# A top-k search whose scores get k's sign once, whose counts read one f32 tensor, and whose small operands lie in PSUM

## The chip, the cores and the metric

The kernel runs on one core of a Trainium2 chip. The core has five engines that each work through a queue of their own in order: TensorE (PE, matrix products into PSUM), VectorE (DVE), ScalarE (ACT), GpSimd (POOL) and SyncE (SP, which issues the transfers). They meet through semaphores. SBUF is the working memory, PSUM the eight banks into which TensorE writes. The metric is the time of one execution on the device in microseconds (us), median of several runs.

## What is computed

The reference is one inference step of a two-layer trunk for 1024 prompt rows and 64 sample rows, 1024 wide. Layer 0 projects the normalised rows into many column tiles; part of them feeds an attention over selected keys, another part a short gated convolution. Layer 1 is a gated unit with a mix over chunks. What matters here is the selection:

```
rel   = relu(einsum('bqhd,bsd->bqhs', qi, ki))
score = einsum('bqh,bqhs->bqs', wi, rel)
score = where(admissible, score, -inf)
top_val, top_idx = top_k(score, topk)        # 256 for the prompt, 144 for the sample
kg, vg = k[top_idx], v[top_idx]              # softmax over the chosen keys alone
```

The kernel never gathers. It finds the k-th largest score of each row exactly and adds 0 to the logits of the chosen keys and -1e30 to the others.

## The kernel before

**Rows and columns.** Scores exist for prompt blocks 2 to 7 (128 rows each, 384 to 1024 columns) and for the sample (576 columns). These seven row blocks lie side by side in one f32 tile `S` of 4800 columns. A column tile of a projection is 72 matrix products: three chunks of 364, 364 and 360 columns, 24 products each (8 pieces of the inner dimension, three products of the exact parts `w_hi`, `w_lo`, `ah`, `al`).

**The search** (`topk`, L488). It walks 31 rounds. In each round every row block counts how many of its scores are smaller than a trial value `cand`, compares the count with a limit (`m`, L571), makes a factor or step from that (`g`, L578 or L588) and moves `cand` (L579 or L590). A row whose k-th largest is negative is searched with its sign turned (`sgn`, +1 or -1 per row). The first 15 rounds (8 for the exponent, 7 for the mantissa) count in `bias`, a bf16 copy of the upper halves of the scores that already carries the sign (L529). The last 16 rounds count in `S` itself and multiply by the sign within the count (L531); there the trial value is a second input, spread over the columns.

**Who counts.** `GROUPS` (L81) makes three groups that go on by themselves. Group 0 (blocks of 512, 640, 768 and 576 columns) is counted by DVE. Group 1 (896 and 1024 columns) is counted by ACT as a sum of signs (L565, L568). Group 2 (384 columns) is counted by DVE in the first 15 rounds and by ACT afterwards. All the small steps are DVE's: three per group and round, on 1 to 4 columns. After the rounds, the blocks that ACT counted are counted once more on DVE (L595), six small steps make the threshold `T` (L598 to L603), and `mask` (L605) writes the additive mask of each block in six DVE instructions (L614 to L619).

**What runs beside it.** While DVE searches, PE computes the column tiles K, V, then GC, XIN and GZ of four convolution tiles (`pj`, L248), then Q1, Q2, Q3 and the first chunk and a half of GB0 as steps (L263; `BEFORE`, L89, is their number, 255 products). ACT copies each finished chunk out of PSUM (L784, L793) into `gc`, `z`, `bo` or `q` and makes `w_hi` of later tiles (L239). POOL makes `w_lo` (L240) and the convolution (L758 to L772). `gc` and `z` have one place each, so a convolution must be over before the next tile is copied there. Chunks rotate through five PSUM banks. Attention (L943 to L958) begins when the masks are there.

**What sets the order.** The order of the instructions within each engine is fixed when the program is built, by a timeline of the builder's own; the engines then run their queues in that order. So an ACT count that waits for a trial value from DVE holds up the copies that stand behind it in ACT's queue, and through the banks PE.

Of the kernel before, what the change touches and what calls it, by code (L numbers as in the profile page):

```python
# [9 lines left out]
F32 = mybir.dt.float32  # L10
# [13 lines left out]
TC = SEQ + 64      # prompt and sample columns  # L24
SO = SEQ           # first sample column
# [7 lines left out]
# chunks of columns: of the projections, and of those back to the residual, where a short one comes last  # L33
# [34 lines left out]
# widths of the score rows: prompt blocks 2..7, then the sample  # L68
# [24 lines left out]
def cut(n):  # L93
    """Equal pieces of at most one bank."""
    k = (n + 511) // 512
    return k, n // k


class Trunk:
# [5 lines left out]
    # ------------------------------------------------------------------ helpers  # L105
# [12 lines left out]
    # ------------------------------------------------------------------ constants  # L118
# [21 lines left out]
    # units of 512 modulation columns: u < 4 hold shift and scale of two k tiles each, 4 and 5 the gate  # L140
# [5 lines left out]
    def ada_steps(self, l, u, raw, halt=False):  # L146
        """A unit, a k tile at a step; with halt another step before the transposition."""
# [26 lines left out]
    def ada_late(self, pool):  # L174
        """The units that the index phase leaves room for, a k tile at a step; their loads run ahead."""
# [25 lines left out]
    def pace(self, after, n):  # L201
        """n steps of the side work, behind one of the matrix products."""
# [40 lines left out]
    def product(self, ps, w, c0, c1, kts=range(KT)):  # L243
        """ps [P, c1-c0] = W^T act, in three products of the exact parts."""
# [6 lines left out]
    def steps(self, w, evac, chunks=range(NCH), n=2, tag="pj"):  # L251
        """A projection, n matrix products at a step."""
# [90 lines left out]
            # 1/rms of every column on all partitions, in place of the sums  # L343
# [55 lines left out]
            # the place of the first tile's weights is free first  # L399
# [833 lines left out]
```

## Time and profile before

| what | value |
| --- | --- |
| time, median of 3 runs (lowest to highest) | 1203.1 us (1202.98 to 1203.14) |
| span of the profiled execution, first to last instruction | 1200.9 us |
| PE busy | 1098.8 us, 91% of the span |
| DVE busy | 729.0 us, 61% |
| ACT busy | 513.6 us, 43% |
| POOL busy | 460.2 us, 38% |
| chain that ended last | PE 61%, DVE 25%, ACT 5%, issue 3%, POOL 2%, DMA 2% |

Only the span of the profiled execution is shown; the 2.2 us between it and the median of the runs lie outside the first and last instruction. A share of busy time hides how long one instruction lasts: the DVE count of 576 columns in line L531 lasts 0.82 us in one round of this trace and 2.82 us in another. So the mean duration of one form, beside its shortest, says more than the share.

### The profile page before, as it was taken

Reading aid. Unit: us, or ns where it says so; the run is one execution under the profiler, and the core shown is the slowest. Engines: PE = TensorE matmul, PEld = TensorE weight load, DVE = VectorE, ACT = ScalarE, POOL = GpSimd, SP = SyncE. Lnnn points to the kernel's source line nnn. Section 1 sums busy time; section 2 is a strip of 40 time slices with the busy share of each in tenths; the row PEclk is TensorE's granted clock in tenths of the full one; section 3 lists DMA queues with packets and bytes.
Section 4 is the critical chain, followed back from the end, with each engine's and each line's share of the span. In section 5 each row is a group of like instructions: output and inputs, shape, how many; then the busy total and the mean of one; then the engine's idle time right before and its main releaser. Section 6 shows DMA issues by size and latency. Waiting matters only on the chain.

```text
span 1200.9 us, 18882 instructions
## 1 busy us (share of the span) xinstructions
PE 1098.8 (91%) x7255; PEld 1054.6 (88%) x7255; DVE 729.0 (61%) x1663; ACT 513.6 (43%) x964; POOL 460.2 (38%) x454
## 2 busy tenths in 40 slices
PE   5899999695959885999999899999999999999997
PEld 4799689595958885988999899999999999999996
DVE  5602899999999798776775534431159036346133
ACT  5332784645665525677775533431221211235110
POOL 3632322344647673544542324641133210245121
PEclk9999999898979896999999899999999999999998
DMA  9646401110101010000000350211111210121012
GB/s 362 279 167 220 168 2 53 73 36 19 36 18 36 19 58 14 19 19 19 19 19 19 114 175 1 71 36 36 36 59 40 84 37 19 52 77 65 1 62 88
DMA packets 26074, 81.84 MB, mean 68 GB/s; under 512 B 3072, under 2 KB 9984, under 8 KB 23552
## 3 DMA queue, kind: packets, MB, share of 16 engines
q1 hardware_dynamic: 25984, 80.63, 19.2%
q8 instruction: 57, 0.93, 0.3%
q14 instruction: 33, 0.27, 0.1%
HBM read 74.50 MB, written 6.12 MB: 67 GB/s over the span
## 4 chain that ended last, share of the span: by engine, by line
PE 61%; DVE 25%; ACT 5%; issue 3%; POOL 2%; DMA 2%; SPq 0%; POOLq 0%; DVEq 0%; ACTq 0%
PE pj L248 26%; PE op L248 15%; DVE cum L531 6%; PE pj L263 6%; DVE cum L529 5%; PE av L670 3%; PE logit_ps L632 3%; PE p_ps L662 2%; DVE m L571 2%; PE ada_ps L154 1%; DVE g L588 1%; PE sgu_ps L1048 1%; DVE cum L616 1%; PE first L319 1%; POOL w_lo L240 1%
## 5 line engine op out<-in xcount | busy, mean ns | idle before, releaser
L248 PE MATMUL pj<-ah,w_hi 128*128 128x364 f32 (+1 forms) x984 | 331.0, 336 | 34.4 <-ACT gc L784 33.0
L248 PE MATMUL pj<-al,w_hi 128*128 128x364 f32 (+1 forms) x984 | 328.3, 334 | 0.0
L248 PE MATMUL pj<-ah,w_lo 128*128 128x364 f32 (+1 forms) x984 | 327.5, 333 | 0.0
L240 POOL TENSOR_TENSOR w_lo<-w_raw,w_hi 128x1024 fp32r<-128x1024 f32 x63 | 160.9, 2556 | 380.8 <-ACT w_hi L239 356.8
L248 PEld LDWEIGHTS pj<-ah,w_hi 128*128 128x128 f32 x984 | 188.8, 192 | 36.6 <-ACT gc L784 33.9
L248 PEld LDWEIGHTS pj<-al,w_hi 128*128 128x128 f32 x984 | 188.8, 192 | 0.0
L248 PEld LDWEIGHTS pj<-ah,w_lo 128*128 128x128 f32 x984 | 188.5, 192 | 0.3 <-issue 0.2
L248 PE MATMUL op<-ah,w_lo 128*128 128x448 f32 (+2 forms) x384 | 126.7, 331 | 3.2 <-POOL w_lo L240 3.2
L248 PE MATMUL op<-al,w_hi 128*128 128x448 f32 (+2 forms) x384 | 127.0, 331 | 0.4 <-DVE al L278 0.3
L248 PE MATMUL op<-ah,w_hi 128*128 128x448 f32 (+2 forms) x384 | 127.3, 331 | 0.0
L239 ACT ACTIVATE w_hi<-w_raw 128x1024 fp32r<-128x1024 f32 x69 | 72.7, 1056 | 108.6 <-PE pj L248 79.1
L988 DVE SCALAR_TENSOR_TENSOR x<-op,mod,x 128x192 f32<-128x192 f32 (+2 forms) x64 | 30.5, 497 | 109.0 <-PE op L248 109.0
L263 PE MATMUL pj<-ah,w_hi 128*128 128x364 f32 (+1 forms) x288 | 96.2, 334 | 0.0
L263 PE MATMUL pj<-al,w_hi 128*128 128x364 f32 (+1 forms) x288 | 95.2, 331 | 0.0
L263 PE MATMUL pj<-ah,w_lo 128*128 128x364 f32 (+1 forms) x288 | 95.2, 331 | 0.0
L639 POOL TENSOR_SCALAR S<-S,sm 128x384 f32<-128x384 f32 (+8 forms) x68 | 50.8, 753 | 85.1 <-DVE sm L638 73.7
L248 PEld LDWEIGHTS op<-ah,w_lo 128*128 128x128 f32 x384 | 73.4, 191 | 5.5 <-POOL w_lo L240 3.5
L531 DVE SCALAR_TENSOR_TENSOR cum<-S,sgn,cand 128x512 bf16<-128x512 f32 (+3 forms) x67 | 76.7, 1145 | 1.5
L248 PEld LDWEIGHTS op<-al,w_hi 128*128 128x128 f32 x384 | 73.3, 191 | 3.2 <-DVE al L278 1.1
L248 PEld LDWEIGHTS op<-ah,w_hi 128*128 128x128 f32 x384 | 73.4, 191 | 2.0
L996 POOL TENSOR_TENSOR acc<-acc,sq 128x448 f32<-128x448 f32 (+2 forms) x40 | 40.0, 999 | 91.4 <-ACT sq L994 90.7
L278 DVE TENSOR_TENSOR ptl<-p_ps,pth 128x512 fp32r<-128x512 f32 (+1 forms) x88 | 54.4, 621 | 20.0 <-ACT pth L277 18.7
(251 smaller groups left out, 2120.1 us busy)
## 6 DMA issues: line engine op xcount, KB each, us to landing
w_raw<-in_w SPq DMA_DIRECT2D x53, 512.0 KB, 3.5
ada<-in_ada_w SPq DMA_DIRECT2D x19, 1024.0 KB, 9.1
w_raw<-in_wo SPq DMA_DIRECT2D x16, 512.0 KB, 3.4
x<-in_x SPq DMA_DIRECT2D x8, 544.0 KB, 6.6
bo<-in_ada_w SPq DMA_DIRECT2D x4, 1024.0 KB, 6.8
x<-in_x SPq DMA_DIRECT2D x1, 1792.0 KB, 8.8
out_y<-x SPq DMA_DIRECT2D x1, 1792.0 KB, 6.6
x<-in_x SPq DMA_DIRECT2D x1, 1536.0 KB, 9.2
```

The costliest lines, as they stand in the source:

```text
L239: nc.scalar.activation(hi, raw, AF.Copy)
L240: (nc.gpsimd if lo_eng == "pool" else nc.vector).tensor_sub(lo, raw, hi)
L248: last = self.nc.tensor.matmul(ps, wt[:, kt, :], at[:, kt, c0:c1], start=n == 0, stop=n == len(mms) - 1)
L263: self.nc.tensor.matmul(ps, wt[:, kt, :], at[:, kt, a:b], start=kt == 0 and i == 0, stop=kt == KT - 1 and i == 2)
L278: (lo_eng or self.nc.vector).tensor_sub(lo, src, hi)
L529: V.tensor_scalar(o, self.bias[:, span(j)], thr, 0.0, op0=OP.is_lt, op1=OP.add, accum_out=col(cv, j))
L531: V.scalar_tensor_tensor(o, self.S[:, span(j)], col(sgn, j), thr.to_broadcast([P, SW[j]]), op0=OP.mult, op1=OP.is_lt, accum_out=col(cv, j))
L632: mm = nc.tensor.matmul(pt[:, 0:w], lhs, keys[i][:, g, s], start=i == 0, stop=i == 1)
L639: nc.gpsimd.tensor_scalar(p, p, st[:, 3:4], 0.0, op0=OP.mult, op1=OP.add)
L670: mm = nc.tensor.matmul(av[:, 0:m], self.vs[0:r, vbase + j, g, :], t[0:r, o:o + m], start=j == 0 and i == 0, stop=j == nj - 1 and i == 1)
L988: nc.vector.scalar_tensor_tensor(x[:, t, a:b], ps[:, a:b], self.mod[l][:, 16 + t, j:j + 1], x[:, t, a:b], op0=OP.mult, op1=OP.add)
L996: nc.gpsimd.tensor_add(acc, acc, sq)
```

## The change

The bf16 copy of the upper halves goes. Once the signs are known, ACT multiplies `S` itself by `sgn`, seven copies in place, in the order of the groups. All 31 rounds then count in `S` in f32 with one form of instruction, a comparison with a scalar per row that adds up its results (`tensor_scalar` with an accumulator). ACT's counts use the constant scale -1 where they had a scale per row (`nsg`, which goes) or the half-step factor. Before the masks, ACT multiplies each block by `sgn` again, which gives the scores back. The limits `limd` and `lima`, the factor `g` and the table `step` move from SBUF to one PSUM bank (tag `av`); `m`, `cv`, `cand` and `T` stay in SBUF.

```
-        cv, m, sgn, nsg, limd, lima, T, cand, g, flag = (
-            t(n) for n in ("cv", "m", "sgn", "nsg", "limd", "lima", "T", "cand", "g", "flag"))
+        cv, m, sgn, limx, T, cand, flag = (t(n) for n in ("cv", "m", "sgn", "limx", "T", "cand", "flag"))
+        small = self.bank("av", "small")
+        limd, lima, g = (small[:, i * NSB:(i + 1) * NSB] for i in range(3))
+        step = small[:, 32:32 + steps * NSB].rearrange("p (s j) -> p s j", j=NSB)
...
-        def smaller(j, thr, first):
-            o = junks[0][:, 0:SW[j]]
-            if first:
-                V.tensor_scalar(o, self.bias[:, span(j)], thr, 0.0, op0=OP.is_lt, op1=OP.add, accum_out=col(cv, j))
-            else:
-                V.scalar_tensor_tensor(o, self.S[:, span(j)], col(sgn, j), thr.to_broadcast([P, SW[j]]),
-                                       op0=OP.mult, op1=OP.is_lt, accum_out=col(cv, j))
+        def smaller(j, thr):
+            V.tensor_scalar(junks[0][:, 0:SW[j]], self.S[:, span(j)], thr, 0.0, op0=OP.is_lt, op1=OP.add,
+                            accum_out=col(cv, j))
...
-        top = self.S.bitcast(BF).rearrange("p (n e) -> p n e", e=2)[:, :, 1]
-        for j in range(NSB):
-            if j in UPPER_ACT:
-                nc.scalar.activation(self.bias[:, span(j)], top[:, span(j)], AF.Copy, scale=col(sgn, j))
-            else:
-                V.tensor_scalar(self.bias[:, span(j)], top[:, span(j)], col(sgn, j), None, op0=OP.mult)
-        V.tensor_scalar(nsg, m, -2.0, 1.0, op0=OP.mult, op1=OP.add)
+        for j in sum((g[0] for g in GROUPS), ()):
+            nc.scalar.activation(self.S[:, span(j)], self.S[:, span(j)], AF.Copy, scale=col(sgn, j))
...
-                elif first:
-                    nc.scalar.activation(junks[1][:, 0:SW[j]], self.bias[:, span(j)], AF.Sign, scale=-1.0 - 2.0 ** -10,
-                                         bias=col(cand, j), accum_out=col(cv, j))
                 else:
-                    nc.scalar.activation(junks[1][:, 0:SW[j]], self.S[:, span(j)], AF.Sign, scale=col(nsg, j),
+                    nc.scalar.activation(junks[1][:, 0:SW[j]], self.S[:, span(j)], AF.Sign, scale=-1.0,
                                          bias=col(cand, j), accum_out=col(cv, j))
...
     def mask(self, pool, j):
+        self.nc.scalar.activation(sl, sl, AF.Copy, scale=self.sgn[:, p])
```

The order of the built program changes at three places that the prediction speaks of. Rows are number, line, operation, output and inputs, columns.

On ACT, the end of the search, before: `junk` are ACT's counts, `gc`, `z` and `q` the copies of finished chunks, and the count in row 227 is the last one.

```order
223 L568 ACTIVATE junk,cv<-S,cand,nsg 128x384
224 L568 ACTIVATE junk,cv<-S,cand,nsg 128x896
225 L568 ACTIVATE junk,cv<-S,cand,nsg 128x1024
226 L793 ACTIVATE z<-pj 128x364
227 L568 ACTIVATE junk,cv<-S,cand,nsg 128x384
228 L239 ACTIVATE w_hi<-w_raw 128x1024
229 L793 ACTIVATE z<-pj 128x296
230 L793 ACTIVATE z<-pj 128x64
231 L784 ACTIVATE q<-pj 128x364 x2
232 L239 ACTIVATE w_hi<-w_raw 128x1024
233 L784 ACTIVATE q<-pj 128x360
234 L784 ACTIVATE q<-pj 128x364 x2
```

And in the changed program: `S<-S,sgn` are the copies that give the scores back, and the last count stands in row 244.

```order
238 L238 ACTIVATE w_hi<-w_raw 128x1024
239 L772 ACTIVATE q<-pj 128x360
240 L601 ACTIVATE S<-S,sgn 128x576
241 L555 ACTIVATE junk,cv<-S,cand 128x896
242 L555 ACTIVATE junk,cv<-S,cand 128x1024
243 L772 ACTIVATE q<-pj 128x364
244 L555 ACTIVATE junk,cv<-S,cand 128x384
245 L601 ACTIVATE S<-S,sgn 128x384
246 L772 ACTIVATE q<-pj 128x364
247 L601 ACTIVATE S<-S,sgn 128x896
248 L601 ACTIVATE S<-S,sgn 128x1024
249 L238 ACTIVATE w_hi<-w_raw 128x1024
```

Before, the last count stood ahead of the last copies of XIN3 (`z`, 296 and 64 columns). Now seven copies of `q` chunks stand ahead of it: all three of Q1 and of Q2, and the first of Q3 (row 243).

On DVE, one round late in the search, before: four counts of group 0 and between them the small steps of all three groups.

```order
516 L531 SCALAR_TENSOR_TENSOR cum,cv<-S,sgn,cand 128x512
517 L531 SCALAR_TENSOR_TENSOR cum,cv<-S,sgn,cand 128x640
518 L531 SCALAR_TENSOR_TENSOR cum,cv<-S,sgn,cand 128x768
519 L531 SCALAR_TENSOR_TENSOR cum,cv<-S,sgn,cand 128x576
520 L571 TENSOR_TENSOR m<-cv,lima 128x2
521 L571 TENSOR_TENSOR m<-cv,limd 128x4
522 L588 SCALAR_TENSOR_TENSOR g<-m,step 128x2
523 L588 SCALAR_TENSOR_TENSOR g<-m,step 128x4
524 L571 TENSOR_TENSOR m<-cv,lima 128x1
525 L590 TENSOR_TENSOR cand<-cand,g 128x2
526 L590 TENSOR_TENSOR cand<-cand,g 128x4
527 L588 SCALAR_TENSOR_TENSOR g<-m,step 128x1
```

And a late round in the changed program, where `small` is the PSUM bank.

```order
535 L528 TENSOR_SCALAR cum,cv<-S,cand 128x512
536 L528 TENSOR_SCALAR cum,cv<-S,cand 128x640
537 L558 TENSOR_TENSOR m<-cv,small 128x2
538 L528 TENSOR_SCALAR cum,cv<-S,cand 128x768
539 L575 SCALAR_TENSOR_TENSOR small<-m,small 128x2
540 L528 TENSOR_SCALAR cum,cv<-S,cand 128x576
541 L577 TENSOR_TENSOR cand<-cand,small 128x2
542 L558 TENSOR_TENSOR m<-cv,small 128x1
543 L575 SCALAR_TENSOR_TENSOR small<-m,small 128x1
544 L577 TENSOR_TENSOR cand<-cand,small 128x1
545 L558 TENSOR_TENSOR m<-cv,small 128x4
```

The number of instructions in a round is the same; each of them now has at most one tensor input in SBUF, and the steps of group 1 stand between the counts of group 0.

On DVE in the masks of the changed program, one product for the convolution branch (`bo<-bo,pj`, the first chunk of GB0) stands in row 575.

```order
573 L603 TENSOR_SCALAR bias<-S,T 128x640
574 L603 TENSOR_SCALAR bias<-S,T 128x768
575 L894 TENSOR_TENSOR bo<-bo,pj 128x364
576 L603 TENSOR_SCALAR bias<-S,T 128x896
577 L603 TENSOR_SCALAR bias<-S,T 128x1024
```

Before, it came behind the last instruction of the masks.

## Rows read from the trace of the kernel before

**Rows 1.** Stages: us, busy time of each engine (instructions), granted clock, DMA.
```profile
187.60:202.00 14.40, 14.38 (x87) 14.35 (x88) 13.55 (x29) 2.90 (x4) 4.62 (x4) 1.00 0.31 104
187.60:444.70 257.10, 211.42 (x1200) 209.60 (x1201) 244.57 (x646) 133.79 (x241) 130.84 (x123) 0.90 0.12 40
461.80:682.50 220.70, 211.97 (x1399) 199.91 (x1399) 156.30 (x481) 156.18 (x330) 99.19 (x95) 0.98 0.08 28
...
412.40:461.00 48.60, 33.80 (x204) 33.35 (x202) 48.25 (x49) 8.81 (x15) 29.27 (x22) 0.88 0.11 36
412.40:429.20 16.80, 16.80 (x103) 16.80 (x102) 16.70 (x24) 3.79 (x6) 15.94 (x17) 1.00 0.10 33
```

**Rows 2.** Waits of PE from 180 to 462: total us, times, longest.
```profile
PE pj L248 <- ACT gc L784: 33.0, 3, 13.0
PE logit_ps L632 <- DVE sm L634: 15.0, 1, 15.0
```

**Rows 3.** Groups on DVE, 180 to 462: busy us, mean ns of one, idle before.
```profile
L531 DVE SCALAR_TENSOR_TENSOR cum<-S,sgn,cand 128x576 bf16<-128x576 f32 x16 | 20.7, 1295 | 0.1
...
L571 DVE TENSOR_TENSOR m<-cv,lima 128x2 f32<-128x2 f32 x31 | 13.0, 418 | 6.4 <-ACT junk L568 6.4
...
L529 DVE TENSOR_SCALAR_CACHE_REDUCE cum<-bias,cand 128x576 bf16<-128x576 bf16 x15 | 12.2, 811 | 0.4
...
L590 DVE TENSOR_TENSOR cand<-cand,g 128x2 f32<-128x2 f32 x22 | 3.5, 157 | 0.1
...
L614 DVE TENSOR_SCALAR_CACHE_REDUCE bias<-S,T,kneg 128x576 bf16<-128x576 f32 x1 | 0.9, 869 | 0.0
```

**Rows 4.** DVE in order of time: start us, us, instruction.
```profile
188.52 0.66 DVE L538 TENSOR_SCALAR sgn<-m 128x7 f32<-128x7 f32 x1
...
202.04 0.75 DVE L529 TENSOR_SCALAR_CACHE_REDUCE cum<-bias,cand 128x512 bf16<-128x512 bf16 x1
...
206.76 0.74 DVE L529 TENSOR_SCALAR_CACHE_REDUCE cum<-bias,cand 128x512 bf16<-128x512 bf16 x1
...
289.93 0.74 DVE L531 SCALAR_TENSOR_TENSOR cum<-S,sgn,cand 128x512 bf16<-128x512 f32 x1
...
304.84 0.75 DVE L531 SCALAR_TENSOR_TENSOR cum<-S,sgn,cand 128x512 bf16<-128x512 f32 x1
...
309.12 0.75 DVE L531 SCALAR_TENSOR_TENSOR cum<-S,sgn,cand 128x512 bf16<-128x512 f32 x1
...
311.90 2.82 DVE L531 SCALAR_TENSOR_TENSOR cum<-S,sgn,cand 128x576 bf16<-128x576 f32 x1
...
314.66 1.95 DVE L571 TENSOR_TENSOR m<-cv,lima 128x2 f32<-128x2 f32 x1
...
385.45 1.75 DVE L531 SCALAR_TENSOR_TENSOR cum<-S,sgn,cand 128x512 bf16<-128x512 f32 x1
...
402.97 0.62 DVE L531 SCALAR_TENSOR_TENSOR cum<-S,sgn,cand 128x384 bf16<-128x384 f32 x1
...
412.43 0.67 DVE L614 TENSOR_SCALAR_CACHE_REDUCE bias<-S,T,kneg 128x384 bf16<-128x384 f32 x1
...
460.80 0.31 DVE L619 TENSOR_SCALAR bias<-bias 128x576 bf16<-128x576 bf16 x1
```

**Rows 5.** POOL in order of time, beside the two long DVE rows of 311.90 and 314.66.
```profile
311.10 3.02 POOL L240 TENSOR_TENSOR w_lo<-w_raw,w_hi 128x1024 fp32r<-128x1024 f32 x1 [11.01 <-ACT w_hi L239]
314.07 2.52 POOL L760 TENSOR_TENSOR z<-z,gc 128x1024 f32<-128x1024 f32 x1
```

**Rows 6.** Line L166, a small DVE sum that reads PSUM: ns shortest, median, longest.
```profile
L166 DVE TENSOR_TENSOR mod<-ada_ps,adab x20: 144/153/167, 23.8 to 149.6; 128x4 f32<-128x4 f32 x16, 128x8 f32<-128x8 f32 x4
```

**Rows 7.** ACT: a group of its counts, and the copy of Q3's first chunk.
```profile
L568 ACT ACTIVATE junk<-S,cand,nsg 128x1024 bf16<-128x1024 f32 x16 | 19.8, 1239 | 0.4
...
430.50 0.48 ACT L784 ACTIVATE q<-pj 128x364 f32<-128x364 f32 x1 [2.70 <-PE pj L263]
```

**Rows 8.** Line L615, the second mask instruction: ns shortest, median, longest.
```profile
L615 DVE TENSOR_SCALAR bias<-S,T x7: 568/1506/1855, 418.8 to 426.8; 128x384 bf16<-128x384 f32 x1, 128x512 bf16<-128x512 f32 x1, 128x640 bf16<-128x640 f32 x1, 128x768 bf16<-128x768 f32 x1
```

More of the change, by code (lines that the diff above doesn't have):

```diff
@@ L83 @@
 COL = {j: n for n, j in enumerate(sum((g[0] for g in GROUPS), ()))}
-UPPER_ACT = (4, 5)
 SPANS = [slice(min(COL[j] for j in g[0]), max(COL[j] for j in g[0]) + 1) for g in GROUPS]
@@ L513, in topk @@
         nc.gpsimd.memset(tiny, 2.0 ** -126)
-        cv, m, sgn, nsg, limd, lima, T, cand, g, flag = (
-            t(n) for n in ("cv", "m", "sgn", "nsg", "limd", "lima", "T", "cand", "g", "flag"))
-        self.T, self.cv = T, cv
+        cv, m, sgn, limx, T, cand, flag = (t(n) for n in ("cv", "m", "sgn", "limx", "T", "cand", "flag"))
+        self.T, self.cv, self.sgn = T, cv, sgn
         junks = [self.cum, pool.tile([P, SEQ], BF, name="junk")]
+        small = self.bank("av", "small")
+        limd, lima, g = (small[:, i * NSB:(i + 1) * NSB] for i in range(3))
+        step = small[:, 32:32 + steps * NSB].rearrange("p (s j) -> p s j", j=NSB)
         def span(j):
@@ L523, in col @@
             return v[:, COL[j]:COL[j] + 1]
-        def smaller(j, thr, first):
-            o = junks[0][:, 0:SW[j]]
-            if first:
-                V.tensor_scalar(o, self.bias[:, span(j)], thr, 0.0, op0=OP.is_lt, op1=OP.add, accum_out=col(cv, j))
-            else:
-                V.scalar_tensor_tensor(o, self.S[:, span(j)], col(sgn, j), thr.to_broadcast([P, SW[j]]),
-                                       op0=OP.mult, op1=OP.is_lt, accum_out=col(cv, j))
+        def smaller(j, thr):
+            V.tensor_scalar(junks[0][:, 0:SW[j]], self.S[:, span(j)], thr, 0.0, op0=OP.is_lt, op1=OP.add,
+                            accum_out=col(cv, j))
         for j in range(NSB):
-            V.tensor_scalar(junks[0][:, 0:SW[j]], self.S[:, span(j)], 0.0, 0.0, op0=OP.is_lt, op1=OP.add,
-                            accum_out=col(cv, j))
+            smaller(j, 0.0)
         V.tensor_tensor(m, cv, lims[:, 1, :], op=OP.is_le)
         V.tensor_scalar(sgn, m, 2.0, -1.0, op0=OP.mult, op1=OP.add)
-        top = self.S.bitcast(BF).rearrange("p (n e) -> p n e", e=2)[:, :, 1]
-        for j in range(NSB):
-            if j in UPPER_ACT:
-                nc.scalar.activation(self.bias[:, span(j)], top[:, span(j)], AF.Copy, scale=col(sgn, j))
-            else:
-                V.tensor_scalar(self.bias[:, span(j)], top[:, span(j)], col(sgn, j), None, op0=OP.mult)
-        V.tensor_scalar(nsg, m, -2.0, 1.0, op0=OP.mult, op1=OP.add)
-        for lim, i in ((limd, 0), (lima, 2)):
-            V.tensor_sub(lim, lims[:, i + 1, :], lims[:, i, :])
-            V.tensor_mul(lim, lim, m)
-            V.tensor_add(lim, lim, lims[:, i, :])
-        for j in range(NSB):
-            smaller(j, col(tiny, j), True)
+        for j in sum((g[0] for g in GROUPS), ()):
+            nc.scalar.activation(self.S[:, span(j)], self.S[:, span(j)], AF.Copy, scale=col(sgn, j))
+        for lim, i in ((limd, 0), (lima, 2)):
+            V.tensor_sub(limx, lims[:, i + 1, :], lims[:, i, :])
+            V.tensor_mul(limx, limx, m)
+            V.tensor_add(lim, limx, lims[:, i, :])
+        for j in sum((g[0] for g in GROUPS), ()):
+            smaller(j, col(tiny, j))
         V.tensor_tensor(flag, cv, limd, op=OP.is_le)
@@ L555, in topk @@
         V.tensor_scalar(cand, tiny, exps[0], None, op0=OP.mult)
-        step = pool.tile([P, steps, NSB], F32, name="step")
         def count(n, first):
@@ L562, in count @@
                 if not act:
-                    smaller(j, col(cand, j), first)
-                elif first:
-                    nc.scalar.activation(junks[1][:, 0:SW[j]], self.bias[:, span(j)], AF.Sign, scale=-1.0 - 2.0 ** -10,
-                                         bias=col(cand, j), accum_out=col(cv, j))
+                    smaller(j, col(cand, j))
                 else:
-                    nc.scalar.activation(junks[1][:, 0:SW[j]], self.S[:, span(j)], AF.Sign, scale=col(nsg, j),
+                    nc.scalar.activation(junks[1][:, 0:SW[j]], self.S[:, span(j)], AF.Sign, scale=-1.0,
                                          bias=col(cand, j), accum_out=col(cv, j))
@@ L594, in topk @@
             if j in ACT_ROWS:
-                smaller(j, col(cand, j), False)
+                smaller(j, col(cand, j))
             else:
```

## The prediction

> **What bounds the kernel now.** I read the stages first, then PE's waits, then DVE's groups by form, and last DVE and POOL side by side in time. PE is the engine that the kernel as a whole is made for: from 461.8 us, where attention begins, to 682.5 it works 211.97 of 220.70 us [rows 1], and nothing in that stage or behind it is touched by the change. The place that can give time is the search and the masks, 188 to 461 us. There DVE is busy 244.57 of 257.10 us and PE only 211.42 [rows 1]. PE waits 33.0 us for ACT's copies of `gc` out of its banks and, once its 255 steps are through, 15.0 us for the masks [rows 2]. ACT is late with `gc` since a count stands ahead of the copy in its queue and waits for DVE's trial value. So DVE sets the pace, directly at the end and through ACT's queue on the way.
>
> DVE is "busy" but not working all the time. An undisturbed round takes 206.76 - 202.04 = 4.72 us among the first 15 and 309.12 - 304.84 = 4.28 among the last 16 [rows 4]. The first 15 took 289.93 - 202.04 = 87.9 us, 17.1 more than 15 x 4.72. The next 15 took 385.45 - 289.93 = 95.5 us, 31.3 more than 15 x 4.28. That is 48 us in which DVE stands. Where: at 311.90 a count that otherwise takes 0.82 us takes 2.82, while POOL's `w_lo` runs from 311.10 to 314.12; the comparison behind it takes 1.95 us, until POOL's next instruction ends at 316.59 [rows 4, 5]. Both forms read two tensors from SBUF, as POOL's do. The count of line L529, with one tensor input and a scalar, does not suffer: its 15 counts of 576 columns have a mean of 811 ns, the 16 of line L531 one of 1295 [rows 3].
>
> **The change, part by part.**
>
> *Counts in f32 by one form.* 67 counts of the two-input form become the form with one input. Is it as fast in f32 as in bf16? Line L614 is this form on f32: 869 ns for 576 columns against 811 in bf16 [rows 3], and it ran while POOL was busy 15.94 of 16.80 us [rows 1]. So I take 0.81 to 0.87 us per 576 columns in every round, at most 7% (0.3 us a round) above the undisturbed one, and no standing.
>
> [...]
>
> *Small operands in PSUM.* Nine of the small steps in a round (`m`, `g`, `cand` for three groups) read or write `limd`, `lima`, `g` or `step`. Each now reads at most one tensor from SBUF, which takes the standing away as it does for the counts: `m` of group 1 has a mean of 418 ns [rows 3], and a sum that reads PSUM never took more than 167 [rows 6]. What does PSUM cost? That sum has a median of 153 ns, one from SBUF alone a mean of 157 [rows 3, 6], so I take nothing more. A write of such a small result to PSUM has no row; bounds: nothing, or another whole duration, 0.16 us.
>
> [...]
>
> *Signs.* Before, `sgn` is ready at 189.2 and the first count of round 1 starts at 202.04 [rows 4]. After, the first of ACT's copies (about 0.7 us) goes ahead of seven counts that start as each block is ready: about 6.8 us by the rates above, the rest of the copies beside them. Round 1 starts near 197, 5 us earlier. On ACT a count loses its scale per row and does not become slower than 1239 ns for 1024 columns [rows 7].
>
> *DVE's sum.* 197 + 15 x 4.72 + 16 x 4.28 = 336 us, and one more ACT round of about 4 for the groups that ACT counts: 340.
>
> *What is late next.* In the new order ACT's last count stands behind the copy of Q3's first chunk, so the search can't end before PE has that chunk. PE needs 14.40 us for 87 products, 0.1655 each [rows 1]. From 187.6 it has 13 tiles of 72, Q1 and Q2 with 144 and 24 of Q3: 1104 products, 182.7 us, and 1 for nine transposes: 371.3 us. That is 31 us behind DVE's sum, so PE paces the search now, and DVE has about 1 us of room in each round. It is also what hides the 0.3 us of the f32 counts, and ACT's seven copies at the start.
>
> PE's standing goes with DVE's: the whole stage has 1200 products and transposes [rows 1], about 198 us, and took 257; 59 us were lost in waits and the slow clock after them (0.90 granted on the mean). 33.0 of them are the three waits on `gc` [rows 2]; these vanish when ACT is ahead. Of the other 26 I leave 3, since the first transposes of V still wait for ACT and DVE (bounds 0 and 26).
>
> *The end.* 371.3 + 3 of waits, 1.3 for copy and last count, then `m`, `g`, `T`, three recounts and six small steps. These took 412.43 - 402.97 = 9.5 us from the recounts on, with two recounts held up; undisturbed about 5.7 with the steps before them. Masks start at 381. They took 48.6 us beside 29.27 us of POOL [rows 1]. Line L615 would need about 7 x 0.57 = 4.0 instead of its mean of 1.2 and more (8.6 in all, seven of them; its shortest is 568 ns [rows 8]); its excess of 4.6 came beside a convolution that by then is over. The other mask lines meet `w_lo` and the query stacks as before. I take 44 (41 to 48.6). The copies that return the scores are finished block by block ahead of the masks, the last two after Q3's second chunk, 4 us behind the first and 6 us ahead of their use. The GB0 product that now stands in the masks needs PE's product 1176, 387 us with the same waits, and is reached at about 390; it adds its 0.5. Attention starts at 425.5 instead of about 461.3 [rows 4]: 36 us.
>
> Behind it PE is full and keeps its 220.7 us [rows 1]; the order there is slightly changed, which I price at 0 (up to 3 either way). Span 1200.9 - 36 = 1165; with the 2.2 us around it: **1167 us**, against the median 1203.1.
>
> **The rivals.**
>
> *PSUM is dear.* Nine steps fit into the room of 1 us per round while each costs under 0.11 us more. At the upper bound, 0.16, DVE's sum grows by 31 x 9 x 0.16 = 45 us, 14 above PE's: 1181. At 0.28 nothing is left of the gain: 1203. The row on reading speaks against it, on writing there is none.
>
> [...]
>
> *Standing stays, the form with one input meets POOL too* when it reads f32. Then 48 us stay on DVE and only the 5 at the start are won: about 1198. L614 beside a busy POOL speaks against it.
>
> *PE keeps part of its waits,* since the convolution on POOL, not the search, holds `gc`: each microsecond kept moves the end by one. With 10 to 26 kept: 1174 to 1190.
>
> *Slower: the search is chained to PE.* Its last count used to need PE's XIN3, and now needs Q3's first chunk. If PE ran as before, that chunk would be copied at 430.5 [rows 7]; count, closing and masks then end at 430.5 + 1.3 + 5.7 + 44 = 482, 20 us later than now: 1223. It decides once more than 39 of PE's 59 lost microseconds stay. For it speaks that the order does put the copy first; against it that the three `gc` waits follow DVE's long rounds.
>
> **How the numbers follow.** The forecast gets 0.72, with a range of its own of 1156 to 1178 (masks 41 to 48.6, PE's waits 0 to 8, 3 for the order behind). PE keeping 10 us or more: 0.12. PSUM dear: 0.06. Standing stays: 0.03. f32 at half the rate: 0.02. Slower through the chain to PE: 0.05. Within 0.2% (about 2.4 us, what a measurement of this kernel can't tell from no change) falls a piece of the last cases and of dear PSUM, 0.03. That makes 0.92 faster, 0.03 the same, 0.05 slower. The range of 1154 to 1187 leaves out the slow end of the rivals, about 0.15, and a little below.
>
> **What would show it.** Right: rounds of 4.7 to 5.9 us with hardly one above 7, no DVE count over 1.1 us; `m` of group 1 under 200 ns; PE without 10 us waits on `gc`, its granted clock near 1.00 from 230 to 385; ACT idle before the copies of chunks, waiting for PE; the last count right behind a `q` copy at 370 to 380; masks done near 425; PE waiting 25 to 35 us for them. Wrong: small steps near 0.3 us each (PSUM), counts of 576 columns near 1.5 us or more (f32 or POOL), PE still 30 us late at its first Q1 chunk.

## The result, and the profile after

The changed kernel takes 1161.8 us (median of four runs, 1160.1 to 1162.2) against 1203.0 for the kernel before on the same chip: a ratio of 0.966, 95% interval 0.964 to 0.967. The forecast was 1167, the range 1154 to 1187. The profiled execution has a span of 1160.5 us, 40.4 less than before.

Four stages, read off DVE's order of time in both traces [rows 4], show where the time came from:

| from, to | before, us | after, us | difference |
| --- | --- | --- | --- |
| start of the signs (`sgn`) to round 1 | 13.52 | 11.57 | -1.95 |
| round 1 to the first recount | 200.93 | 174.64 | -26.29 |
| first recount to the first mask instruction | 9.46 | 4.39 | -5.07 |
| masks, to the first logits of attention | 49.04 | 38.57 | -10.47 |

That is 43.8 us. The stretch ahead of the signs, where the code is the same, took 2.3 us longer in this execution (190.84 against 188.52), and the time from the first logits to the end 1.1 longer (740.49 against 739.43): 40.4 remain.

DVE of the changed kernel in order of time: start us, us, instruction.

```profile
190.84 0.67 DVE L534 TENSOR_SCALAR sgn<-m 128x7 f32<-128x7 f32 x1
191.43 0.78 DVE L540 TENSOR_TENSOR limx<-limx,m 128x7 f32<-128x7 f32 x1
192.24 2.35 DVE L541 TENSOR_TENSOR small<-limx,lims 128x7 f32<-128x7 f32 x1
...
194.91 0.74 DVE L528 TENSOR_SCALAR_CACHE_REDUCE cum<-S,tiny 128x512 bf16<-128x512 f32 x1
...
202.41 0.75 DVE L528 TENSOR_SCALAR_CACHE_REDUCE cum<-S,cand 128x512 bf16<-128x512 f32 x1
...
365.57 0.75 DVE L528 TENSOR_SCALAR_CACHE_REDUCE cum<-S,cand 128x512 bf16<-128x512 f32 x1
...
375.31 0.16 DVE L558 TENSOR_TENSOR m<-cv,small 128x2 f32<-128x2 f32 x1 [5.17 <-ACT junk L555]
...
377.05 0.61 DVE L528 TENSOR_SCALAR_CACHE_REDUCE cum<-S,cand 128x384 bf16<-128x384 f32 x1
...
381.44 0.67 DVE L602 TENSOR_SCALAR_CACHE_REDUCE bias<-S,T,kneg 128x384 bf16<-128x384 f32 x1
...
420.01 0.28 DVE L622 CUSTOM_DVE_ANT_0 S<-logit_ps,corner 128x128 f32<-128x128 f32 x1
```

The reader is to see three things. The masks start at 381.44, the forecast's 381. Two small steps that read two tensors from SBUF still stand at the start (line L540 for 0.78 us, and L541 for 2.35; their second pair, some 3 us later, takes 0.17 each). And at the end of the search DVE waits 5.17 us for ACT's last counts. The groups on DVE (busy us, mean ns of one, idle before) show that the counts and the small steps no longer stand in the rounds:

```profile
L528 DVE TENSOR_SCALAR_CACHE_REDUCE cum<-S,cand 128x576 bf16<-128x576 f32 x31 | 25.1, 811 | 0.0
...
L558 DVE TENSOR_TENSOR m<-cv,small 128x2 f32<-128x2 f32 x31 | 4.8, 155 | 19.7 <-ACT junk L555 19.4
...
L575 DVE SCALAR_TENSOR_TENSOR small<-m,small 128x4 f32<-128x4 f32 x23 | 3.8, 165 | 0.5
```

The f32 count of 576 columns takes 811 ns, to the nanosecond what the bf16 count took [rows 3]; `m` of group 1 takes 155 instead of 418. What DVE lost to standing it now partly waits for ACT: 19.7 us ahead of `m`. PE's stages (busy time of each engine, granted clock, DMA) and its waits from 180 to 470:

```profile
187.60:390.30 202.70, 201.72 (x1217) 201.25 (x1215) 173.74 (x627) 140.18 (x255) 117.09 (x125) 1.00 0.15 51
390.30:421.90 31.60, 0.94 (x4) 0.50 (x2) 29.68 (x36) 2.02 (x6) 2.87 (x3) 0.56 0.00 0
...
400.00:420.00 20.00, 0.00 (x0) 0.00 (x0) 19.79 (x21) 0.14 (x1) 0.00 (x0) 0.50 0.00 0
...
381.44:420.00 38.56, 9.01 (x57) 8.80 (x55) 38.25 (x50) 4.07 (x7) 8.22 (x5) 0.66 0.05 17
420.00:641.50 221.50, 211.74 (x1399) 199.03 (x1399) 156.00 (x484) 157.36 (x334) 97.46 (x95) 0.98 0.08 28
```

```profile
PE logit_ps L620 <- DVE sm L622: 31.9, 2, 29.9
PE pj L247 <- ACT w_hi L238: 1.0, 1, 1.0
```

PE works 201.72 of 202.70 us at a granted clock of 1.00, where before it lost some 59 us in this stage at 0.90 on the mean [rows 1]; the three waits on `gc` [rows 2] are gone. In their place stand 31.9 us of waiting for the masks, 29.9 of them in one piece, in which PE does nothing; from 400 to 420 the granted clock is 0.50.

### The profile page after: what moved, and what is told of

Its sections match the earlier page's. It is cut to its first block, busy times and chain, and to the rows that moved or that the text cites. A ratio compares the mean times of both kernels' runs of the same rounds, so it can differ in the third digit from the quotient of the medians.

```text
span 1160.5 us, 18892 instructions
## 1 busy us (share of the span) xinstructions
PE 1087.5 (94%) x7255; PEld 1044.7 (90%) x7255; DVE 670.2 (58%) x1657; ACT 519.3 (45%) x976; POOL 440.1 (38%) x454
## 3 DMA queue, kind: packets, MB, share of 16 engines
q1 hardware_dynamic: 25984, 80.63, 19.7%
## 4 chain that ended last, share of the span: by engine, by line
PE 81%; DVE 7%; ACT 5%; POOL 3%; issue 3%; DMA 1%; SPq 0%; POOLq 0%; DVEq 0%; ACTq 0%
PE pj L247 40%; PE op L247 15%; PE pj L262 9%; PE av L658 3%; PE logit_ps L620 2%; PE p_ps L650 2%; PE ada_ps L153 2%; PE sgu_ps L1036 1%; PE score_ps L427 1%; PE first L318 1%; POOL w_lo L239 1%; POOL hf L329 1%; DVE cum L604 1%; PE score_ps L428 1%; DVE al L277 1%
## 5 line engine op out<-in xcount | busy, mean ns | idle before, releaser
L247 PE MATMUL pj<-ah,w_hi 128*128 128x364 f32 (+1 forms) x984 | 326.0, 331 | 1.0 <-ACT w_hi L238 1.0
L247 PE MATMUL pj<-al,w_hi 128*128 128x364 f32 (+1 forms) x984 | 323.8, 329 | 0.0
L247 PE MATMUL pj<-ah,w_lo 128*128 128x364 f32 (+1 forms) x984 | 323.1, 329 | 0.0
L239 POOL TENSOR_TENSOR w_lo<-w_raw,w_hi 128x1024 fp32r<-128x1024 f32 x63 | 158.0, 2510 | 341.3 <-ACT w_hi L238 336.4
L247 PEld LDWEIGHTS pj<-ah,w_hi 128*128 128x128 f32 x984 | 185.0, 188 | 2.0 <-ACT w_hi L238 1.3
L247 PEld LDWEIGHTS pj<-ah,w_lo 128*128 128x128 f32 x984 | 184.8, 188 | 0.3 <-issue 0.2
L247 PEld LDWEIGHTS pj<-al,w_hi 128*128 128x128 f32 x984 | 185.0, 188 | 0.0
L528 DVE TENSOR_SCALAR_CACHE_REDUCE cum<-S,cand 128x512 bf16<-128x512 f32 (+5 forms) x142 | 119.0, 838 | 2.0
L262 PE MATMUL pj<-ah,w_hi 128*128 128x364 f32 (+1 forms) x288 | 96.0, 334 | 0.0
L262 PE MATMUL pj<-ah,w_lo 128*128 128x364 f32 (+1 forms) x288 | 95.2, 330 | 0.0
L262 PE MATMUL pj<-al,w_hi 128*128 128x364 f32 (+1 forms) x288 | 95.1, 330 | 0.0
L555 ACT ACTIVATE junk<-S,cand 128x896 bf16<-128x896 f32 (+2 forms) x78 | 77.7, 996 | 24.4 <-DVE m L558 20.6
L620 PE MATMUL logit_ps<-kp,qst 128*128 128x384 f32 (+5 forms) x192 | 49.6, 366 | 33.2 <-DVE sm L622 32.6
```

What stands on the lines that cost most here:

```text
L239: (nc.gpsimd if lo_eng == "pool" else nc.vector).tensor_sub(lo, raw, hi)
L247: last = self.nc.tensor.matmul(ps, wt[:, kt, :], at[:, kt, c0:c1], start=n == 0, stop=n == len(mms) - 1)
L262: self.nc.tensor.matmul(ps, wt[:, kt, :], at[:, kt, a:b], start=kt == 0 and i == 0, stop=kt == KT - 1 and i == 2)
L528: V.tensor_scalar(junks[0][:, 0:SW[j]], self.S[:, span(j)], thr, 0.0, op0=OP.is_lt, op1=OP.add, accum_out=col(cv, j))
L555: nc.scalar.activation(junks[1][:, 0:SW[j]], self.S[:, span(j)], AF.Sign, scale=-1.0, bias=col(cand, j), accum_out=col(cv, j))
L620: mm = nc.tensor.matmul(pt[:, 0:w], lhs, keys[i][:, g, s], start=i == 0, stop=i == 1)
```

## The experiments

Each kernel ran beside the kernel before on the same chip, so ratios compare best; the changed kernel has 0.9657 (0.9643 to 0.9671).

| kernel | median us | ratio, 95% interval |
| --- | --- | --- |
| after, small operands in SBUF | 1184.0 | 0.9833 (0.9815 to 0.9850) |
| before, small operands in PSUM | 1182.4 | 0.9822 (0.9807 to 0.9836) |
| after, late counts with two SBUF inputs | 1176.8 | 0.9772 (0.9753 to 0.9791) |
| before, `w_lo` twice | 1238.6 | 1.0289 (1.0274 to 1.0304) |
| after, `w_lo` twice | 1169.4 | 0.9729 (0.9716 to 0.9743) |
| after, return copies on POOL | 1159.4 | 0.9646 (0.9629 to 0.9663) |
| after, 120 products ahead | 1175.0 | 0.9771 (0.9749 to 0.9793) |
| after, second mask instruction adds up | 1161.0 | 0.9656 (0.9643 to 0.9669) |
| after, 320 products ahead | 1157.0 | 0.9625 (0.9612 to 0.9638) |
| after, masks late | 1159.1 | 0.9632 (0.9612 to 0.9652) |
| after, masks late, 320 products ahead | 1156.6 | 0.9603 (0.9581 to 0.9625) |

**Which of the two parts removes the standing.** First the changed kernel with its small operands back in SBUF.

```
-        small = self.bank("av", "small")
+        small = pool.tile([P, 200], F32, name="small")
```

> The changed kernel with limd, lima, g and step back in SBUF; counts and signs stay as changed. Theory (a small step with two tensors in SBUF stands while POOL reads SBUF): in the kernel before, the small steps of a round took about 35 us more in all than at 0.15 to 0.17 us each; that comes back. The comparison m of group 1 has a mean of 300 ns or more (155 in the changed kernel), the counts keep 0.81 us per 576 columns, DVE becomes the pacer again, masks start 8 to 25 us after 381, time 1168 to 1185 us. Rival (the standing belonged to the two-input counts, small steps only queued behind them): m under 200 ns, time within 4 us of 1161.8.

```profile
L528 DVE TENSOR_SCALAR_CACHE_REDUCE cum<-S,cand 128x576 bf16<-128x576 f32 x31 | 25.0, 806 | 0.1
L558 DVE TENSOR_TENSOR m<-cv,small 128x2 f32<-128x2 f32 x31 | 13.1, 424 | 3.3 <-ACT junk L555 3.3
L575 DVE SCALAR_TENSOR_TENSOR small<-m,small 128x2 f32<-128x2 f32 x23 | 12.8, 557 | 0.0
```

These are its groups on DVE. `m` is back at 424 ns, the counts are untouched at 806; 22 us of the gain are gone and the masks start at 402.33. The theory's numbers hold; the standing was not the counts' alone. With the counts out of the way more of it falls on the small steps: `m`, `cand` and `g` of the last 23 rounds take 82 us in all here, 68 in the kernel before and 39 in the changed one.

Then the kernel before with only its small operands in PSUM (and two more small tiles for the limits):

```
+        small = self.bank("av", "small")
+        limd, lima, g = (small[:, i * NSB:(i + 1) * NSB] for i in range(3))
+        step = small[:, 32:32 + steps * NSB].rearrange("p (s j) -> p s j", j=NSB)
```

> The kernel before with limd, lima, g and step in a PSUM bank; counts as before (bf16 in 15 rounds, two SBUF inputs in 16). Theory: small steps fall to 0.15 to 0.17 us each, the two-input counts of line L531 keep their standing (576 columns about 1.2 to 1.3 us), so some 30 of 48 us leave DVE's search; what is left of the gain is bounded by PE: 1166 to 1182 us. Rival (each POOL instruction stops DVE once, whatever stands there, so the standing moves from the small steps into the counts): the 576-column counts of the second stage rise to 1.8 us or more and the time stays at 1190 to 1203. Rival (PSUM operands are dear): small steps at 0.25 us or more.

```profile
L533 DVE SCALAR_TENSOR_TENSOR cum<-S,sgn,cand 128x576 bf16<-128x576 f32 x16 | 22.6, 1415 | 0.0
L533 DVE SCALAR_TENSOR_TENSOR cum<-S,sgn,cand 128x768 bf16<-128x768 f32 x16 | 21.6, 1348 | 0.1
...
L573 DVE TENSOR_TENSOR m<-cv,small 128x2 f32<-128x2 f32 x31 | 4.7, 151 | 3.6 <-ACT junk L570 2.3 <-ACT junk L567 0.8
```

Small steps fall to 151 ns, and PSUM is not dear. But the time came out at the edge of what I expected (1182.4), because the counts got longer than I had put them: 1415 ns against 1295 [rows 3]. The four forms of the late counts take 80.2 us together; at the changed kernel's means (747, 878, 1010 and 811 ns, 16 each) they need 55.1. So 25 us stand there, where the kernel before had 15 (70.0 in all). The first rival's numbers (1.8 us a count, 1190 us or more) did not come, but it was right in part: 10 us of the standing that the small steps no longer catch are caught by the next instructions with two SBUF inputs.

Third, the changed kernel with two-input counts in the last 16 rounds alone:

```
-                    smaller(j, col(cand, j))
+                    smaller(j, col(cand, j), not first)
+            if two: return V.scalar_tensor_tensor(junks[0][:, 0:SW[j]], self.S[:, span(j)], 1.0, thr.to_broadcast([P, SW[j]]), op0=OP.mult, op1=OP.is_lt, accum_out=col(cv, j))
```

> The changed kernel, but the counts of the last 16 rounds (and no others) in the form with two SBUF inputs, the trial value spread over the columns, on the same f32 scores that already carry the sign. Theory: these counts stand beside POOL again, 576 columns with a mean of 1.0 us or more (0.81 in the changed kernel), some 10 to 20 us of DVE in all; the small steps stay at 0.15 to 0.17 us; PE and ACT hide part of it: 1164 to 1174 us. Rival (the sign factor, not the second input, made the old counts slow): mean under 0.85 us and 1160 to 1163 us.

```profile
L527 DVE SCALAR_TENSOR_TENSOR cum<-S,cand 128x576 bf16<-128x576 f32 x16 | 25.4, 1587 | 0.0
L527 DVE SCALAR_TENSOR_TENSOR cum<-S,cand 128x768 bf16<-128x768 f32 x16 | 24.8, 1548 | 0.1
```

1587 ns against 811 on the same scores, with no sign in it: the second input made the counts slow, not the sign. The four forms take 80.2 us here too. Undisturbed, the two-input form is no slower: its shortest 576-column count takes 0.76 us here and 0.81 in the kernel before. 15 us of the time come back, 3 more than I expected at most.

**POOL as the cause.** Both kernels with `w_lo` computed twice for each tile fetched during the search:

```
+        for _ in range(2 if self.twice else 1): (nc.gpsimd if lo_eng == "pool" else nc.vector).tensor_sub(lo, raw, hi)
```

> The kernel before, but POOL makes w_lo of each column tile fetched in the search twice, some 14 more instructions of about 2.5 us, 36 us more on POOL. Theory (POOL reading SBUF makes DVE stand): DVE's two-input groups get longer, about 15 us more in all by the ratio of 48 us of standing to some 115 of POOL, and the time is 1210 to 1230 us. Rival (the long DVE rows only happen to lie beside POOL): mean durations of DVE's forms as before, time within 5 us of 1203.

> The changed kernel with the same second w_lo on POOL for each column tile fetched in the search, some 17 more instructions, 41 us more on POOL. Theory (DVE has no instruction with two SBUF inputs left in the rounds): the counts keep 0.81 us per 576 columns and the small steps 0.15 to 0.17; the time stays within 4 us of 1161.8 unless POOL itself comes late with the convolution. Rival (any DVE instruction meets POOL): counts or small steps longer by over 10 percent in the mean, time 1170 or more.

Groups on DVE of the kernel before with `w_lo` twice, then of the changed one:

```profile
L531 DVE SCALAR_TENSOR_TENSOR cum<-S,sgn,cand 128x576 bf16<-128x576 f32 x16 | 19.6, 1223 | 0.1
...
L588 DVE SCALAR_TENSOR_TENSOR g<-m,step 128x2 f32<-128x2 f32 x23 | 12.5, 542 | 0.1
```

```profile
L528 DVE TENSOR_SCALAR_CACHE_REDUCE cum<-S,cand 128x576 bf16<-128x576 f32 x31 | 25.1, 810 | 0.0
L558 DVE TENSOR_TENSOR m<-cv,small 128x2 f32<-128x2 f32 x31 | 4.8, 154 | 13.3 <-ACT junk L555 12.9
L605 DVE SCALAR_TENSOR_TENSOR bias<-cum,bias 128x768 bf16<-128x768 bf16 x1 | 3.2, 3165 | 0.0
L604 DVE TENSOR_TENSOR_SCAN cum<-ones,cv,bias 128x896 bf16<-128x896 f32 x1 | 3.1, 3085 | 0.0
```

The changed kernel's rounds don't notice 12 more `w_lo` (29 of 2.40 us up to 381, against 17 of 2.41): 810 and 154 ns, and its masks start at 380.92. The 7.6 us that it loses lie behind the search: the convolution comes later and now meets the masks, whose two-input instructions stand (line L605 at 768 columns, 3.17 us where the changed kernel took 0.95); from the first mask instruction to the first logits it takes 46.07 us instead of 38.57. My bound of 4 us held only if POOL did not come late with the convolution, and it did. The kernel before loses 35 us, more than expected. The way was right, the price was not: `g` of group 1 goes from 359 to 542 ns, but the 576-column count gets no longer (1223), and PE waits 55.9 us for ACT's copies of `z`. The four stages of the profiled executions (1237.8 us against 1200.9) divide the loss: 6.5 us from the signs to round 1, 13.4 in the rounds, 1.3 to the masks, 9.5 in the masks, 5.9 behind the first logits and 0.3 ahead of the signs. In the rounds DVE is busy 203.3 of 214.3 us where it was 189.8 of 200.9, with the same 569 instructions, so those 13.4 us are standing, and they fall on the small steps: `cand` of group 1 goes from 157 [rows 3] to 339 ns, while the four forms of the late counts take 70.8 us where they took 70.0. The 15.4 us from the masks on come with a convolution that is later; what of them is standing is not separated.

**What sets the end of the search now.** Return copies on POOL instead of ACT:

```
-        self.nc.scalar.activation(sl, sl, AF.Copy, scale=self.sgn[:, p])
+        self.nc.gpsimd.tensor_scalar(sl, sl, self.sgn[:, p], 0.0, op0=OP.mult, op1=OP.add)
```

> The changed kernel, but POOL instead of ACT gives the scores their sign back ahead of the masks. In ACT's queue the last counts then stand ahead of the copy of Q3's first chunk, with no return copies before them. Theory A (the search's end follows PE, through the weights and the copy that ACT must wait for at 371): the end of the search moves by 1 us or less, and 1160 to 1164 us, the POOL copies lying beside DVE's masks. Theory B (ACT's own queue with 4 us of return copies ahead of the last counts sets the end): 1156 to 1159.

Ahead of ACT's last counts now stands this wait, in ACT's order of time (in brackets the idle time before it and what ended it):

```profile
369.29 1.06 ACT L238 ACTIVATE w_hi<-w_raw 128x1024 fp32r<-128x1024 f32 x1 [2.81 <-POOL gc L759]
```

`w_hi` goes into the place that tile Q2 leaves. The profile names POOL's `gc` as the releaser, which ended at 369.04; I take PE for it, since `w_hi` starts 0.41 us after PE's last product with Q2's `w_hi` begins, here (368.88) as in the changed kernel (370.49 and 370.90). From the first count of round 1 to the finished threshold it takes 178.9 us (200.66 to 379.55), in the changed kernel 178.75: nothing is won, as theory A said. DVE's wait for the last counts does shrink, from 5.17 to 4.50 us, but one closing step (line L586) now takes 1.05 us beside the copies on POOL instead of 0.16. The medians can't be told apart.

The other side: fewer products ahead of attention.

```
-BEFORE = 255
+BEFORE = 120
```

> The changed kernel with 120 instead of 255 products ahead of attention, so that neither the weights that wait for Q2's end nor the copies of Q2's last and Q3's first chunk stand ahead of ACT's last counts. Theory (PE's chunks in ACT's queue set the end of the search in the changed kernel): from the first count of round 1 to the finished threshold 175 to 176 us, 3 to 4 less than the 178.8 of the changed kernel. Rival (DVE's and ACT's own counts set it): 178 or more. The 135 products come back inside attention: 10 to 22 us, so 1167 to 1182 us in all by either.

176.7 us (199.80 to 376.47): 2.1 less, between theory and rival. With PE's chunks and weights out of the way, three return copies (2.31 us) stand right ahead of ACT's last counts, and DVE still waits 3.09 us instead of 5.17; with the return copies out of the way it waited 4.50. So neither alone is "the" bound; both at once were not taken away. The 135 products come back in attention as expected (1175.0).

**The masks.** The second mask instruction with an accumulator:

```
-        V.tensor_scalar(bi, sl, thr, None, op0=OP.is_equal)
+        V.tensor_scalar(bi, sl, thr, 0.0, op0=OP.is_equal, op1=OP.add, accum_out=self.cv2[:, p])
```

> The changed kernel, but the second mask instruction (line L603) also adds up its result, so that it is the form that line L602 and the counts have. In the changed kernel its seven take 8.6 us beside POOL's query stacks, where the shortest suggest 4.0 without them; L602 takes 0.67 to 1.33 us for the same columns and did not suffer. Theory: the seven take about 6.9 us wherever POOL is, so 1.5 to 2 us are won: 1159.5 to 1160.5. Rival (POOL holds this form up as well): 8.6 or more, no gain.

ns shortest, median, longest of the seven, first in the changed kernel, then in this one:

```profile
L603 DVE TENSOR_SCALAR bias<-S,T x7: 414/741/1750, 387.8 to 394.6; 128x384 bf16<-128x384 f32 x1, 128x512 bf16<-128x512 f32 x1, 128x640 bf16<-128x640 f32 x1, 128x768 bf16<-128x768 f32 x1
```

```profile
L604 DVE TENSOR_SCALAR_CACHE_REDUCE bias<-S,T x7: 609/875/1278, 385.9 to 391.5; 128x384 bf16<-128x384 f32 x1, 128x512 bf16<-128x512 f32 x1, 128x640 bf16<-128x640 f32 x1, 128x768 bf16<-128x768 f32 x1
```

The form with the accumulator costs 195 ns more at its shortest (384 columns) and shows no standing (its longest is that of 1024 columns), while the one without does (768 columns took 1750 ns, 1024 took 741), though both read one tensor from SBUF. Why the two forms differ is not shown. The 8.6 us of my expectation was a misreading: the seven take 6.91 us in the changed kernel (8.61 was before), and 6.10 here with the reading of the accumulators. That is the 0.8 us by which the masks are shorter (38.0 us from threshold to first logits instead of 38.85); in the median it can't be told from nothing. The form that adds up did not stand beside POOL's query stacks (768 columns took 1.01 us there), but the gain is too small to matter.

**Using PE's 30 us of idling.** More products ahead of attention, GB2 ahead of GA0 in the list of tiles:

```
-BEFORE = 255
+BEFORE = 320
-... (GB, 0), (GB, 1), (GA, 0), (GB, 2), (GA, 1), (GB, 3), (GA, 2), (GA, 3)]
+... (GB, 0), (GB, 1), (GB, 2), (GA, 0), (GB, 3), (GA, 1), (GA, 2), (GA, 3)]
```

> The changed kernel with 65 more projection products ahead of attention (BEFORE 320 in place of 255), and GB2 placed ahead of GA0 in the list of tiles. PE waits 30 us for the masks in the changed kernel; 65 products of 0.1655 us are 10.8 us of work that leave the attention stage. Theory (attention is bound by PE): 10.8 less some 1.6 for three more products of DVE in the masks and up to 3 for w_lo beside the masks: 1152 to 1156. Rival (attention is held by its chain over ACT, DVE and POOL): within 3 us of 1161.8, or slower by the 2 to 5 us in the masks.

The first interval that is, just, clear of the changed kernel's: some 4 us, less than expected. The masks take 42.5 us from the threshold (379.40 to 421.89), 3.6 more, with three more products on DVE and one more `w_lo` beside them. And attention is not PE's alone:

```profile
421.90:641.50 219.60, 205.35 (x1344) 192.61 (x1345) 157.37 (x482) 156.53 (x334) 94.40 (x94) 0.97 0.08 25
```

PE is busy 205.35 of 219.60 us there, against 211.74 of 221.50: it idles 4.5 us more, so of the 10.8 us taken out that much comes back as waits there and 3.6 in the masks.

Masks written just ahead of the attention block that needs their place:

```
+MASKS = {0: (0,), 1: (1,), 2: (2,), 3: (3, 4), 4: (5,), 5: (6,)}
-                for j in range(NSB):
-                    self.mask(se, j)
                     for b in ORDER[t]:
+                        for j in MASKS.get(b, ()) if t == 0 else ():
+                            self.mask(ap, j)
                         self.attend(ap, st, t, b)
```

> The changed kernel, but each block's mask is written into the program just ahead of the first attention block whose scores need its place, in place of all seven ahead of attention; the first two attention blocks use no mask at all. In the built order the first logits then stand behind 17 mask instructions on DVE and not behind all 42. Theory (since the change the path runs from the search over DVE's masks to attention, and PE idles 30 us of it; attention itself has room on DVE, 156 of 221.5 us busy): attention starts about 22 us earlier, of which up to 10 are given back where the remaining 22 us of masks push DVE's work in the first head pair: 1138 to 1152 us. Rival (DVE sets the first head pair's pace then, all is given back): 1156 to 1164.

> The kernel with late masks and also 320 products ahead of attention with GB2 ahead of GA0. PE idles only about 8 us then, so 65 products (10.8 us) more than fill it. Theory: the gain of more products ahead and the gain of late masks are the same idle time, so the sum is not more than 3 us better than late masks alone, and may be slower. Rival (they add up): 5 us better or more.

Three stretches of the changed kernel, and the same of the one with late masks:

```profile
381.00:420.00 39.00, 9.45 (x59) 9.24 (x57) 38.54 (x52) 4.50 (x8) 8.22 (x5) 0.67 0.05 17
420.00:440.00 20.00, 17.64 (x95) 16.02 (x96) 15.01 (x63) 16.76 (x44) 11.07 (x17) 0.80 0.08 20
440.00:480.00 40.00, 38.45 (x261) 35.38 (x259) 29.89 (x91) 26.62 (x55) 20.53 (x19) 1.00 0.04 15
```

```profile
381.00:420.00 39.00, 21.89 (x108) 19.33 (x106) 37.58 (x75) 14.47 (x35) 18.88 (x15) 0.76 0.07 24
420.00:440.00 20.00, 15.03 (x76) 13.39 (x74) 18.23 (x43) 7.65 (x16) 10.25 (x5) 0.78 0.00 1
440.00:480.00 40.00, 39.12 (x261) 35.57 (x261) 29.87 (x96) 27.95 (x58) 20.99 (x22) 1.00 0.09 28
```

The first logits come 17.8 us behind the threshold instead of 38.85, as expected. But DVE is as full as before (37.58 of 39 us), now with masks and attention in turn, and its last mask instruction comes at 437.33. PE has done 184 products by 440 instead of 154, at a granted clock below 0.8; the rest is given back, as the rival said: DVE paces the first head pair. Of PE's waits from 381 to 440, 10.3 us are for DVE's sums and 9.9 for POOL's scaling of `S`, which itself waits for DVE's sums. Both edits together give 1156.6 us, the fastest kernel here: its interval is clear of the changed kernel's (some 6 us by the ratios), but overlaps those of either edit alone, so whether they add up stays open.

## Why the prediction was right

*Standing.* The core of it: DVE's instructions with two tensors in SBUF stood while POOL worked, both the counts (1295 ns on the mean for 576 columns [rows 3], 811 with one) and the small steps (`m` of group 1 418 ns [rows 3], 155 with its limits in PSUM). The first three experiments show the parts, the doubled `w_lo` that POOL is behind it: 13.4 us more in the rounds of the kernel before, nothing in those of the changed one. The counts with one SBUF input took 811 and 810 ns with POOL's `w_lo` once and twice. What it is in the two engines that makes the one wait for the other, no run shows. One step that I had not counted among them stood too: `g` of the first 8 rounds (for the exponent) reads a single tensor, in a `tensor_scalar` without an accumulator. Group 1's took 509 ns on the mean with its result in SBUF and 158 with it in PSUM (with it in SBUF 336 in the changed kernel and 161 in the kernel before with `w_lo` twice, so 509 is no fixed price). Before, then after:

```profile
L578 DVE TENSOR_SCALAR g<-m 128x2 f32<-128x2 f32 x8 | 4.1, 509 | 0.0
```

```profile
L565 DVE TENSOR_SCALAR small<-m 128x2 f32<-128x2 f32 x8 | 1.3, 158 | 0.0
```

*f32 counts.* I allowed 0.81 to 0.87 us; they took 0.811. No run shows the half rate to which I gave 0.02: the f32 count took what the bf16 count took, 811 ns [rows 3]. A gain that no run isolates lies beside them: ACT's count of 1024 columns takes 1149 ns with the constant scale, 1239 with one per row [rows 7].

*PSUM.* 150 to 165 ns a step, reads and writes alike; that rival falls too, and with PE's three waits gone, so do the one on PE keeping them and the slower one that needed them. (One price of the PSUM rival was summed wrongly: by its own terms 0.28 us a step gives 1214, and 1203 is reached at 0.24.)

*Signs.* Wrong in size: I gained 5 us to round 1, the trace 1.95. My sum went from the signs to the counts and left out the limits between them: lines L540 and L541 take 3.1 us beside POOL, where their second pair takes 0.34. It cost nothing in the end: the search did not wait for DVE's sum, as the next point shows.

*PE paces the search.* Right in the engine, wrong in the wait. PE was held up for 1.0 us in all (I had left 3); it was busy 201.72 us, where I had 198 for 1200 instructions and it now runs 1217. ACT's last count ended at 376.24, 0.6 behind my 375.6. But it was not the end of Q3's first chunk that held the last counts, as I put it:

```profile
370.90 1.06 ACT L238 ACTIVATE w_hi<-w_raw 128x1024 fp32r<-128x1024 f32 x1 [0.65 <-issue]
371.87 0.45 ACT L772 ACTIVATE q<-pj 128x360 f32<-128x360 f32 x1
372.22 0.77 ACT L601 ACTIVATE S<-S,sgn 128x576 f32<-128x576 f32 x1
372.88 1.03 ACT L555 ACTIVATE junk<-S,cand 128x896 bf16<-128x896 f32 x1
...
375.19 0.46 ACT L772 ACTIVATE q<-pj 128x364 f32<-128x364 f32 x1
375.54 0.60 ACT L555 ACTIVATE junk<-S,cand 128x384 bf16<-128x384 f32 x1
```

ACT idles ahead of `w_hi`, by the reading above until PE leaves Q2's weights, and from there it works without a gap until the last count is over. PE finishes Q3's first chunk at about 375.0, but ACT comes to its copy at 375.19, straight from a count. So the wait that sets the end is that for PE's end of Q2, 24 products earlier than I had it, and behind it stands ACT's own queue: the next weights, a chunk of Q2, a return copy and two counts. That this queue (4.3 us) is about as long as the 24 products (4.0), and the end so near my figure, is luck. I had the return copies down as done ahead of the masks and priced them at nothing; one stands in that queue, and taking them off ACT shortened DVE's wait by 0.7 us.

*Closing steps.* 5.7 us forecast from the last count to the masks, 5.2 measured (376.24 to 381.44).

*Masks.* The term that was mis-sized: 44 us forecast and 0.5 for the GB0 product, 38.57 measured with it, below the 41 that I had as the least. These 5.9 us are more than all that lies between 1167 and 1161.8 (5.2). I credited one line (L615) with 4.6 us that it would lose when the convolution is over, and left the rest as it was. It went the other way round. That line lost only 1.7 (8.61 to 6.91 us), since POOL's query stacks (6.04 us from 386.48) now run beside it; the other 8.8 of the 10.5 us come from the lines behind it, which before met the query stacks and two `w_lo` and now are free: POOL is busy 8.22 us in the masks instead of 29.27 [rows 1]. An example is the scan of 512 columns, before and after:

```profile
L616 DVE TENSOR_TENSOR_SCAN cum<-ones,cv,bias 128x512 bf16<-128x512 f32 x1 | 3.4, 3412 | 0.0
```

```profile
L604 DVE TENSOR_TENSOR_SCAN cum<-ones,cv,bias 128x512 bf16<-128x512 f32 x1 | 1.3, 1277 | 0.0
```

(The forecast's own range, 1156 to 1178, is that of the span; with the 2.2 us around it, its terms give 1158 to 1180.)

## What to carry to other kernels

When two engines work side by side, read the mean duration of one instruction form against its shortest before believing a busy share: some 48 us of DVE's 244 were standing. What decided here was the second SBUF input (and, in the masks and in `g`, the `tensor_scalar` without accumulator), so a scalar operand (1295 to 811 ns a count) or a PSUM bank for a few columns (418 to 155 ns a step) was enough to get out of the way; get all forms out of it: with the small steps alone out, the late counts stood 10 us longer than before. When a bound falls, look for a second cause behind it before paying for the first.

## What was not expected of the hardware

It went both ways: POOL stood too. POOL's multiplication of 512 columns by a scalar in the convolution (`tap`), from 205 to 370 us, in the changed kernel, the one with only its small operands in SBUF, the one with two-input late counts, and the kernel before:

```profile
L758 POOL TENSOR_SCALAR tap<-z,convw 128x512 f32<-128x512 f32 x16 | 11.2, 700 | 0.8
```

```profile
L758 POOL TENSOR_SCALAR tap<-z,convw 128x512 f32<-128x512 f32 x12 | 8.3, 693 | 0.6
```

```profile
L758 POOL TENSOR_SCALAR tap<-z,convw 128x512 f32<-128x512 f32 x14 | 12.3, 880 | 0.7
```

```profile
L770 POOL TENSOR_SCALAR tap<-z,convw 128x512 f32<-128x512 f32 x9 | 8.2, 908 | 0.4
```

Beside DVE's long two-input counts the mean is 880 and 908 ns, without them 700 and 693. Small steps with two SBUF inputs made DVE stand (424 ns) and left POOL as it was (693 ns). Whether these shorter POOL instructions helped to bring the convolution forward, out of the masks, is not shown: in the changed kernel POOL's `w_lo` still waits 65.5 us of that stretch for ACT's `w_hi`.
